# Binary cross entropy on one core: from tiles with a separate output to two fixed rings worked on in place

## The chip, the cores and the metric

The kernel runs on one core of a Trainium2 chip. Time is the device time of one execution in microseconds (us), median of ten runs; the profile is one further look at a single execution. The engines that matter are VectorE (DVE), ScalarE (ACT), GpSimd (POOL, here only the issuer of transfers), SyncE (SP, the issuer of a few) and the 16 DMA engines between HBM and SBUF.

## The reference

```python
"pred":   np.random.uniform(0.01, 0.99, (8192, 8192)).astype(np.float32)
"target": np.random.randint(0, 2, (8192, 8192)).astype(np.float32)

def reference(pred, target):
    eps = 1e-7
    pred = np.clip(pred, eps, 1 - eps)
    return -(target * np.log(pred) + (1 - target) * np.log(1 - pred))
```

Every target is 0 or 1, so only one of the two logarithms counts: that of |pred + target - 1|, which is pred where the target is 1 and 1 - pred where it is 0. Both inputs and the result are float32, 268.4 MB each.

## The kernel before

The matrix is walked in 64 blocks of 128 rows, one row to an SBUF partition, 8192 columns each: a block of pred or of the result is 4.19 MB, 32 KiB in one piece per partition. Pred comes into tiles `t_p` (float32, three buffers), target into `t_t` (bfloat16, two buffers, converted on the way by the transfer), and the result leaves from `t_o` (fp16, two buffers), converted to float32 by the transfer.

For each block, `ops` issues four instructions over the whole 8192 columns: DVE forms pred - 1 + target in place (L70); ACT squares it in place (L73) and takes the logarithm in place (L74); DVE multiplies by -0.5 into `t_o` (L75). The half undoes the square. There is no clip.

The order is that of the loop. Block `bi` first issues its pred load (L116; L114 on SP for block 0) and its target load (L117) on the GpSimd queue, then the store of block `bi - 2` (L63), then its arithmetic. GpSimd issues these transfers one after another and waits ahead of each until its buffer is free: the pred load until L75 of three blocks before has read the tile, the target load until L70 of two blocks before has read the tile, the store until L75 has written `t_o`. The last two blocks go through `ops_tail` in 4 and 8 pieces (L87, L95, L96, L97), in place in `t_p`, with stores from SP (L100).

Of the kernel before, what the change touches and what calls it, by code (L numbers as in the profile page):

```python
# [1 line left out]

# [4 lines left out]


@with_exitstack
def kernel(  # L10
    ctx: ExitStack,
    tc: tile.TileContext,
    pred: bass.AP,
    target: bass.AP,
    out: bass.AP,
):
    nc = tc.nc
    fp32 = mybir.dt.float32
    fp16 = mybir.dt.float16
    bf16 = mybir.dt.bfloat16  # L20

    P = nc.NUM_PARTITIONS

    pred_f = pred.flatten_outer_dims()
    target_f = target.flatten_outer_dims()
    out_f = out.flatten_outer_dims()

    R, C = pred_f.shape

    F = 8192 if C % 8192 == 0 else C  # L30
    n_col = C // F
    n_row = (R + P - 1) // P
    n_blk = n_row * n_col

    big = (R % P == 0) and n_blk >= 8 and F == 8192

    sub = mybir.AluOpType.subtract
    add = mybir.AluOpType.add
    mult = mybir.AluOpType.mult

    Square = mybir.ActivationFunctionType.Square
    Ln = mybir.ActivationFunctionType.Ln

    pool_p = ctx.enter_context(tc.tile_pool(name="bce_p", bufs=3 if big else 2))
    pool_t = ctx.enter_context(tc.tile_pool(name="bce_t", bufs=2))
    pool_o = ctx.enter_context(tc.tile_pool(name="bce_o", bufs=2))
    pool_w = ctx.enter_context(tc.tile_pool(name="bce_w", bufs=1))

    warm = pool_w.tile([1, 8], fp32, name="warm", tag="warm")
    nc.vector.memset(warm, 1.0)  # L50
    nc.scalar.activation(out=warm, in_=warm, func=Ln)  # L51

    lb = n_blk - 1
    slb = n_blk - 2

    pending: dict[int, list] = {}

    def emit_store(b: int, n: int | None = None):
        lst = pending[b]
        n = len(lst) if n is None else n  # L60
        for _ in range(n):
            dram, sl = lst.pop(0)
            nc.gpsimd.dma_start(out=dram, in_=sl)  # L63
        if not lst:
            del pending[b]

    def ops(bi, rows, r0, g0, t_p, t_t):
        t_o = pool_o.tile([P, F], fp16, name="t_o", tag="t_o")
        p_sl = t_p[:rows]
        nc.vector.scalar_tensor_tensor(  # L70
            out=p_sl, in0=p_sl, scalar=1.0, in1=t_t[:rows], op0=sub, op1=add
        )
        nc.scalar.activation(out=p_sl, in_=p_sl, func=Square)  # L73
        nc.scalar.activation(out=p_sl, in_=p_sl, func=Ln)  # L74
        nc.vector.tensor_scalar(  # L75
            out=t_o[:rows], in0=p_sl, scalar1=-0.5, scalar2=None, op0=mult
        )
        pending.setdefault(bi, []).append(
            (out_f[r0 : r0 + rows, g0 : g0 + F], t_o[:rows])
        )  # L80

    def ops_tail(rows, r0, g0, t_p, t_t, nchunk):
        W = F // nchunk
        for k in range(nchunk):
            c0 = k * W
            p_sl = t_p[:rows, c0 : c0 + W]
            nc.vector.scalar_tensor_tensor(  # L87
                out=p_sl,
                in0=p_sl,
                scalar=1.0,  # L90
                in1=t_t[:rows, c0 : c0 + W],
                op0=sub,
                op1=add,
            )
            nc.scalar.activation(out=p_sl, in_=p_sl, func=Square)  # L95
            nc.scalar.activation(out=p_sl, in_=p_sl, func=Ln)  # L96
            nc.vector.tensor_scalar(  # L97
                out=p_sl, in0=p_sl, scalar1=-0.5, scalar2=None, op0=mult
            )
            nc.sync.dma_start(  # L100
                out=out_f[r0 : r0 + rows, g0 + c0 : g0 + c0 + W], in_=p_sl
            )

    for bi in range(n_blk):
        i, j = divmod(bi, n_col)
        r0 = i * P
        rows = min(P, R - r0)
        g0 = j * F

        t_p = pool_p.tile([P, F], fp32, name="t_p", tag="t_p")  # L110
        t_t = pool_t.tile([P, F], bf16 if big else fp32, name="t_t", tag="t_t")

        if big and bi == 0:
            nc.sync.dma_start(out=t_p[:rows], in_=pred_f[r0 : r0 + rows, g0 : g0 + F])  # L114
        else:
            nc.gpsimd.dma_start(out=t_p[:rows], in_=pred_f[r0 : r0 + rows, g0 : g0 + F])  # L116
        nc.gpsimd.dma_start(out=t_t[:rows], in_=target_f[r0 : r0 + rows, g0 : g0 + F])  # L117

        s = bi - 2
        if s in pending:  # L120
            emit_store(s)

        if big and bi == slb:
            ops_tail(rows, r0, g0, t_p, t_t, 4)
        elif big and bi == lb:
            ops_tail(rows, r0, g0, t_p, t_t, 8)
        else:
            ops(bi, rows, r0, g0, t_p, t_t)

    for b in sorted(pending):  # L130
        emit_store(b)


# [1 line left out]
_INS = ['pred', 'target']  # L135
_OUTS = [((8192, 8192), 'float32')]


# [23 lines left out]
```

## Time and profile before

| what | value |
|---|---|
| median of 10 runs | 1867.65 us (1867.37 to 1867.91) |
| the profiled execution | 1867.91 us, of which the profile's span is 1866.2 us |
| L70, DVE, 128x8192, 62 times | 8.693 us each, 538.9 us in all |
| L73 and L74, ACT, 128x8192, 62 times each | 7.029 us each, 435.8 us in all for each line |
| L75, DVE, 128x8192, float32 to fp16, 62 times | 4.427 us each, 274.4 us in all |
| a transfer's issue on GpSimd | 0.53 to 0.54 us |
| median from issue to landing | pred load 49.3 us, target load 49.0 us, store 40.2 us |

Busy time is that of the engine; the idle time that a group shows is the time of its engine just before it, with the event that ended it. DMA has no instruction rows of its own: its busy share is in the slices of the span, the rate of a stretch in the windows, and the time from issue to landing in the list of issues.

### The profile page before, as it was taken

The page shows a single profiled execution, that of the slowest core. Times are in us where ns is not written, and L with a number is a line of the kernel's source. Part 1 is how long each engine was busy: PE and PEld are TensorE (multiplying, and loading weights), DVE is VectorE, ACT ScalarE, POOL GpSimd, SP SyncE. Part 2 cuts the span into 40 slices and gives each one's busy share as a digit, 9 for nine tenths or more (in the row PEclk, how much of TensorE's full clock was granted, in tenths as well). Part 3 has the DMA queues.
Part 4 walks back from the last instruction along what each step waited for, and adds up shares of the span by engine and source line. Part 5 has one row for each costly group of instructions (what it writes and reads, how often), then busy time and mean ns, then how long its engine had stood idle before and what let it go on. Part 6 is the DMA issues. An engine that isn't in the chain of part 4 may idle for free.

```text
span 1866.2 us, 804 instructions
## 1 busy us (share of the span) xinstructions
DVE 841.3 (45%) x149; ACT 903.3 (48%) x150; POOL 100.6 (5%) x193
## 2 busy tenths in 40 slices
DVE  2545344453443534435344353453534535345353
ACT  3653644535445354453544535446354463553654
POOL 0000000000000000000000000000000000000000
DMA  9999999999999999999999999999999999999999
GB/s 326 337 376 354 349 381 343 376 358 345 386 339 376 355 347 383 346 367 363 343 388 346 363 369 340 391 340 363 370 344 386 345 359 371 347 379 352 352 379 350
DMA packets 29094, 671.14 MB, mean 360 GB/s; under 512 B 3233, under 2 KB 3233, under 8 KB 4257
## 3 DMA queue, kind: packets, MB, share of 16 engines
q0 software_dynamic: 27216, 658.52, 99.9%
q1 hardware_dynamic: 1872, 12.58, 1.7%
q14 instruction: 6, 0.04, 0.0%
HBM read 536.87 MB, written 268.44 MB: 432 GB/s over the span
## 4 chain that ended last, share of the span: by engine, by line
DMA 81%; issue 15%; ACT 2%; DVE 1%; another core or an unknown queue 1%; POOL 0%; POOLq 0%; DVEq 0%; PEldq 0%
DMA t_t<-in_target_dram 81%; ACT t_p L96 1%; ACT t_p L95 1%; DVE t_p L70 0%; DVE t_o L75 0%; DVE t_p L87 0%; DVE t_p L97 0%; POOL t_p L116 0%; POOL t_t L117 0%; POOL out_dram L63 0%; POOLq L117 0%; POOLq L63 0%; DVEq L87 0%; DVEq L70 0%
## 5 line engine op out<-in xcount | busy, mean ns | idle before, releaser
L73 ACT ACTIVATE t_p<-t_p 128x8192 f32<-128x8192 f32 x62 | 435.8, 7029 | 924.1 <-DVE t_p L70 924.1
L75 DVE TENSOR_SCALAR t_o<-t_p 128x8192 f16<-128x8192 f32 x62 | 274.4, 4427 | 845.0 <-ACT t_p L74 845.0
L70 DVE SCALAR_TENSOR_TENSOR t_p<-t_p,t_t 128x8192 f32<-128x8192 f32 x62 | 538.9, 8693 | 145.3 <-DMA t_t<-in_target_dram 145.3
L74 ACT ACTIVATE t_p<-t_p 128x8192 f32<-128x8192 f32 x62 | 435.8, 7029 | 2.0
L63 POOL DMA_DIRECT2D out_dram<-t_o x62 | 33.3, 537 | 1122.3 <-DVE t_o L75 1101.7
L117 POOL DMA_DIRECT2D t_t<-in_target_dram x64 | 34.0, 531 | 581.8 <-DVE t_p L70 581.0
L116 POOL DMA_DIRECT2D t_p<-in_pred_dram x63 | 33.8, 536 | 0.3 <-issue 0.3
L95 ACT ACTIVATE t_p<-t_p 128x1024 f32<-128x1024 f32 (+1 forms) x12 | 15.6, 1328 | 26.5 <-DVE t_p L87 26.5
L87 DVE SCALAR_TENSOR_TENSOR t_p<-t_p,t_t 128x1024 f32<-128x1024 f32 (+1 forms) x12 | 18.4, 1575 | 17.2 <-DMA t_t<-in_target_dram 17.2
L96 ACT ACTIVATE t_p<-t_p 128x1024 f32<-128x1024 f32 (+1 forms) x12 | 15.6, 1330 | 0.1
L97 DVE TENSOR_SCALAR t_p<-t_p 128x1024 f32<-128x1024 f32 (+1 forms) x12 | 10.3, 869 | 7.9 <-ACT t_p L96 7.9
L51 ACT ACT_TABLE_LOAD x1 | 1.3, 1283 | 0.7 <-PEq L146 0.7
L50 DVE MEMSET warm<- 1x8 f32 x1 | 0.1, 65 | 0.8 <-PEq L146 0.8
L51 ACT ACTIVATE warm<-warm 1x8 f32<-1x8 f32 x1 | 0.2, 207 | 0.0
L146 POOL MEMSET const-float32-0.0<- 128x1 f32 x1 | 0.1, 100 | 0.3 <-issue 0.3
L146 POOL MEMSET const-bfloat16-1.0<- 128x1 bf16 x1 | 0.1, 102 | 0.0
L146 POOL MEMSET const-float32-1.0<- 128x1 f32 x1 | 0.1, 100 | 0.0
L146 POOL MEMSET const-uint8-127<- 128x1 uint8 x1 | 0.1, 100 | 0.0
## 6 DMA issues: line engine op xcount, KB each, us to landing
t_p<-in_pred_dram POOLq DMA_DIRECT2D x63, 4096.0 KB, 49.3
out_dram<-t_o POOLq DMA_DIRECT2D x62, 4096.0 KB, 40.2
t_t<-in_target_dram POOLq DMA_DIRECT2D x64, 2048.0 KB, 49.0
t_p<-in_pred_dram SPq DMA_DIRECT2D x1, 4096.0 KB, 19.4
out_dram<-t_p SPq DMA_DIRECT2D x4, 1024.0 KB, 27.3
out_dram<-t_p SPq DMA_DIRECT2D x8, 512.0 KB, 8.5
```

The costliest lines, as they stand in the source:

```text
L51: nc.scalar.activation(out=warm, in_=warm, func=Ln)
L63: nc.gpsimd.dma_start(out=dram, in_=sl)
L70: nc.vector.scalar_tensor_tensor(out=p_sl, in0=p_sl, scalar=1.0, in1=t_t[:rows], op0=sub, op1=add)
L73: nc.scalar.activation(out=p_sl, in_=p_sl, func=Square)
L74: nc.scalar.activation(out=p_sl, in_=p_sl, func=Ln)
L75: nc.vector.tensor_scalar(out=t_o[:rows], in0=p_sl, scalar1=-0.5, scalar2=None, op0=mult)
L87: nc.vector.scalar_tensor_tensor(out=p_sl, in0=p_sl, scalar=1.0, in1=t_t[:rows, c0 : c0 + W], op0=sub, op1=add,)
L95: nc.scalar.activation(out=p_sl, in_=p_sl, func=Square)
L96: nc.scalar.activation(out=p_sl, in_=p_sl, func=Ln)
L97: nc.vector.tensor_scalar(out=p_sl, in0=p_sl, scalar1=-0.5, scalar2=None, op0=mult)
L116: nc.gpsimd.dma_start(out=t_p[:rows], in_=pred_f[r0 : r0 + rows, g0 : g0 + F])
L117: nc.gpsimd.dma_start(out=t_t[:rows], in_=target_f[r0 : r0 + rows, g0 : g0 + F])
```

## The change

The matrix is taken as one flat run. A chunk of width w is 128 x w consecutive elements, partition p holding w of them in a row. Widths are 4096, 4096, 8192, then 30 times 16384 (64 KiB per partition in float32), then 8192, 4096, 2048, 1024, 1024; together 524288 columns.

In SBUF there are two tiles for the whole run: `ring_p`, 32768 columns of float32, and `ring_t`, 32768 columns of bfloat16. Chunk k lies at its start column modulo 32768. The result replaces pred in `ring_p` and is stored from there as float32. All transfers but the first pred load are issued on the GpSimd queue. `load_what_fits` issues the target and the pred load of each next chunk as far as the ring has room behind the last chunk whose store was issued.

The arithmetic runs in pieces of 2048 columns (1024 in the two last chunks). `front` is clip and subtraction on DVE, Abs and Ln on ACT; `back` is a multiplication by -1 on DVE. The loop issues `front` of piece i, then `back` of piece i - 2; when that was the last piece of its chunk, it issues the chunk's store and what can be loaded then. The order on each engine is that of the loop.

```diff
+RING = 32768
+SUB = 2048
+LAG = 2
+def chunk_widths(total):
+    head = [4096, 4096, 8192]
+    tail = [8192, 4096, 2048, 1024, 1024]
+    big = 16384
...
-    pool_p = ctx.enter_context(tc.tile_pool(name="bce_p", bufs=3 if big else 2))
-    pool_t = ctx.enter_context(tc.tile_pool(name="bce_t", bufs=2))
-    pool_o = ctx.enter_context(tc.tile_pool(name="bce_o", bufs=2))
+    ring_p = pool.tile([P, RING], fp32, name="ring_p", tag="ring_p")
+    ring_t = pool.tile([P, RING], bf16, name="ring_t", tag="ring_t")
...
+    def load_t(k):
+        c, w = at(k), widths[k]
+        nc.gpsimd.dma_start(out=ring_t[:, c : c + w], in_=dram(target_f, cols[k], w))
+    def load_p(k):
+        c, w = at(k), widths[k]
+        queue = nc.sync if k == 0 else nc.gpsimd
+        queue.dma_start(out=ring_p[:, c : c + w], in_=dram(pred_f, cols[k], w))
+    def store(k):
+        c, w = at(k), widths[k]
+        nc.gpsimd.dma_start(out=dram(out_f, cols[k], w), in_=ring_p[:, c : c + w])
...
-        nc.vector.scalar_tensor_tensor(
-            out=p_sl, in0=p_sl, scalar=1.0, in1=t_t[:rows], op0=sub, op1=add
-        )
-        nc.scalar.activation(out=p_sl, in_=p_sl, func=Square)
-        nc.scalar.activation(out=p_sl, in_=p_sl, func=Ln)
-        nc.vector.tensor_scalar(
-            out=t_o[:rows], in0=p_sl, scalar1=-0.5, scalar2=None, op0=mult
-        )
+    def front(c, w):
+        p, t = ring_p[:, c : c + w], ring_t[:, c : c + w]
+        nc.vector.tensor_scalar(
+            out=p, in0=p, scalar1=EPS, scalar2=1 - EPS, op0=Alu.max, op1=Alu.min
+        )
+        nc.vector.scalar_tensor_tensor(
+            out=p, in0=t, scalar=1.0, in1=p, op0=Alu.subtract, op1=Alu.add
+        )
+        nc.scalar.activation(out=p, in_=p, func=Act.Abs)
+        nc.scalar.activation(out=p, in_=p, func=Act.Ln)
+    def back(c, w):
+        p = ring_p[:, c : c + w]
+        nc.vector.tensor_scalar(
+            out=p, in0=p, scalar1=-1.0, scalar2=None, op0=Alu.mult
+        )
...
+    def load_what_fits():
+        nonlocal loaded
+        while (
+            loaded < len(widths)
+            and cols[loaded] + widths[loaded] <= (cols + [total])[stored] + RING
+        ):
+            load_t(loaded)
+            load_p(loaded)
+            loaded += 1
+    with tc.manual_schedule():
+        load_what_fits()
+        nc.vector.memset(warm, 1.0)
+        nc.scalar.activation(out=warm, in_=warm, func=Act.Ln)
+        for i in range(len(pieces) + LAG):
+            if i < len(pieces):
+                _, c, w, _ = pieces[i]
+                front(c, w)
+            if i >= LAG:
+                k, c, w, last = pieces[i - LAG]
+                back(c, w)
+                if last:
+                    store(k)
+                    stored = k + 1
+                    load_what_fits()
```

## The prediction

> **What bounds the kernel now.** I read the page first, from the totals to the engines.
>
> ```profile
> span 1866.2 us, 804 instructions
> DVE 841.3 (45%) x149; ACT 903.3 (48%) x150; POOL 100.6 (5%) x193
> DMA  9999999999999999999999999999999999999999
> q0 software_dynamic: 27216, 658.52, 99.9%
> HBM read 536.87 MB, written 268.44 MB: 432 GB/s over the span
> ```
>
> DVE and ACT are busy for less than half of the span; the 16 DMA engines are full in every slice. The reads and writes of HBM add up to 805.3 MB, and no byte of that can go: the two inputs and the result are float32 on the HBM side. So the limit is the flow of transfers, and what counts in the change is whether the flow is ever interrupted. Next, the windows of one undisturbed stretch (its length, the busy time of DVE, ACT and GpSimd, the clock, the DMA share and the rate) and the timeline of a block (start, length, engine and line, and in brackets the idle time before it with what ended that) give the rate and the rhythm:
>
> ```profile
> 1748.11:1806.12 58.01, 26.24 (x5) 28.12 (x4) 2.65 (x5) 1.00 1.02 361
> ```
> ```profile
> 758.50 0.54 POOL L63 DMA_DIRECT2D out_dram<-t_o  x1 [18.05 <-DVE t_o L75]
> 759.03 0.54 POOL L116 DMA_DIRECT2D t_p<-in_pred_dram  x1
> 759.98 8.69 DVE L70 SCALAR_TENSOR_TENSOR t_p<-t_p,t_t 128x8192 f32<-128x8192 f32 x1 [1.77 <-DMA t_t<-in_target_dram]
> 768.70 7.03 ACT L73 ACTIVATE t_p<-t_p 128x8192 f32<-128x8192 f32 x1 [14.95 <-DVE t_p L70]
> 768.96 0.53 POOL L117 DMA_DIRECT2D t_t<-in_target_dram  x1 [9.39 <-DVE t_p L70]
> ...
> 782.82 4.43 DVE L75 TENSOR_SCALAR t_o<-t_p 128x8192 f16<-128x8192 f32 x1 [14.16 <-ACT t_p L74]
> 787.54 0.54 POOL L63 DMA_DIRECT2D out_dram<-t_o  x1 [18.06 <-DVE t_o L75]
> 789.03 8.69 DVE L70 SCALAR_TENSOR_TENSOR t_p<-t_p,t_t 128x8192 f32<-128x8192 f32 x1 [1.78 <-DMA t_t<-in_target_dram]
> ```
>
> A block starts every 789.03 - 759.98 = 29.05 us; over the long stretch 29.03. It carries 3 x 4.19 MB on the HBM side, so 12.58 MB / 29.03 us = 433 GB/s (the window's 361 counts the target at its two bytes in SBUF). All 64 blocks at this pace are 64 x 29.03 = 1857.9 us of the 1866.2. The rest is the start (the window view shows the first packets at about 1.75 us), the way from the last packet to the end (the rate collapses near 1863.1, so 3.1 us), and some 3.5 us of small losses. The timeline also shows why there is no hole: the table "us to landing" puts a target load at 49.0 us from issue to landing although its share of the flow is below 10 us, so transfers stand in line well ahead of the engines. Last, the groups by shape give prices for 2048 columns:
>
> ```profile
> L87 DVE SCALAR_TENSOR_TENSOR t_p<-t_p,t_t 128x2048 f32<-128x2048 f32 x4 | 9.0, 2287 | 1.7 <-DMA t_t<-in_target_dram 1.7
> L95 ACT ACTIVATE t_p<-t_p 128x2048 f32<-128x2048 f32 x4 | 7.5, 1898 | 8.5 <-DVE t_p L87 8.5
> L97 DVE TENSOR_SCALAR t_p<-t_p 128x2048 f32<-128x2048 f32 x4 | 4.9, 1226 | 4.7 <-ACT t_p L96 4.7
> ```
>
> **What the Trainium skill says.** "DMA: Bandwidth & Descriptors", section Where 436 GB/s comes from, puts the ceiling of one core's transfers at 435.2 GB/s; the 433 here agrees, so longer runs have nothing left to win. The same page, Latency and other measured facts, warns of lost rate at row pitches of large powers of two, but its table still has full rate at 512 KiB (207 of 214 GB/s); the change goes from 32 to 64 KiB. The trace shows only 32 KiB and below. "SBUF — State Buffer", section SBUF: two separate sides, says that GpSimd can't write the descriptors of its transfers while a two-port VectorE instruction runs, and that such a transfer starts after that instruction. Before, no store is issued inside such an instruction, so this trace doesn't show it.
>
> **The change, part by part.**
>
> 1. Bytes. The store now reads float32 in SBUF in place of fp16, but wrote float32 to HBM before too. The side that limits stays 4 bytes per element: 805.3 MB as before. Change 0; by the ceiling at best 1857.9 - 805.3/0.4352 = 7.5 us could be won, and I take 0.
>
> 2. Compute. Per piece of 2048 columns DVE does clip, subtract and negate. The clip is a new form; it has one source as L97 has, so I take 1.226 us (if it ran at one element per cycle as L87 does, 2.287). Sum 1.226 + 2.287 + 1.226 = 4.74 us, for 256 pieces 1213 us. ACT: 2 x 1.90 = 3.80 us, 973 us; Abs is priced as Square. Both stay below the 58.06 us that the flow needs per 16384 columns: DVE 8 x 4.74 = 37.9, ACT 30.4. Hidden, as throughput. The activation table is still loaded once.
>
> 3. Buffers. Before, three pred tiles, two target tiles and two separate outputs let loads run on while a block is computed and stored. After, the pred ring holds 32768 columns, that is two big chunks, and the result stays in its place. Chunk k+2 can be loaded only where chunk k was, after its store. The target load of k+2 and the pred load of k+2 are issued behind store(k) on the one GpSimd queue. The pred load waits for the store to land, which costs nothing: the target load of k+2, 8.39 MB on the HBM side, takes 8.39/0.433 = 19.4 us and flows meanwhile.
>
> 4. The order on DVE, where it goes wrong. The loop issues front(i) and only then back(i-2). The last two negations of chunk k stand behind clip and subtract of pieces 0 and 1 of chunk k+1, and the first of those clips waits for the pred load of k+1. DVE runs in order. So store(k) can't be issued until load k+1 has landed, and behind store(k) stand the loads of k+2. In the moment in which load k+1 lands nothing is left in the DMA queues. The flow stops, once per chunk. Without the lag the two negations could have been done some 12 us before, since chunk k needs 37.9 us of DVE and about 8 us for its last pieces on ACT after its own load has landed, and the next three transfers take 58 us.
>
> The hole, step by step: last packet to DVE's start 1.4 us (block 0 of before: 8.39 MB for its two loads from 1.75 us take 19.35, that is to 21.1; DVE starts at 22.52). Then clip, subtract, negate, clip, subtract, negate: 2 x 4.74 = 9.5 us (hops between them are 0.02 to 0.05 in the chain of waits, and overlaps of 0.06 stand against them). DVE to GpSimd 0.3 (55.05 to 55.34). From the issue to the first packet: SP's first transfer took 1.0 us (0.75 to 1.75); the GpSimd instruction is 0.54 where SP's is 0.37, and descriptors are written by software, so 1.5, bounds 1.0 and 2.5. Then the descriptor stall: right behind the negation DVE starts the next clip, 1.226 us; bounds 0 and 2.5 (the page's stall of a short copy), taken 0.5. Sum 1.4 + 9.5 + 0.3 + 1.5 + 0.5 = 13.2 us. Bounds 12.2 (no stall, fast issue) to 16.2; with a clip at one element per cycle 2.1 more.
>
> 5. How many holes. Chunks 0 to 2 are the head (16384 columns), 3 to 32 are big, 33 to 37 are the tail. At the start chunks 0 to 3 are loaded in one go; stores 0 and 1 (4.84 us each) stand behind load 3 and cover 9.7 us of the first hole, leaving 3.5. After the loads of chunks 4 to 32 the hole is whole: 29 of them, 29 x 13.2 = 383 us. The tail has none: store(31) is followed by 38.7 us of tail loads, the first of which lands early enough for store(32), and compute of the tail (7 x 4.74 + 2 x 2.6 = 38 us) is done before its 38.7 us of stores. Short rows cost there under 1 us, as the last slices still move 414 to 426 GB/s.
>
> Sum: 1.75 + 1857.9 + 383 + 3.5 + 3.1 = 2249 us of span. The profiled execution was 1867.91 for a span of 1866.2, 1.7 more, and the median 1867.65 is within 0.3 of it. So 2251. Where before had 3.5 us of small losses, I keep none; that is inside the range.
>
> **Rivals.**
>
> A (forecast, 0.80): holes of 12 to 15 us per chunk, about 2250.
>
> B (0.10): larger holes, because the clip isn't as quick as L97 (2 x 1.06 = 2.1 us a hole) or descriptors wait longer behind DVE. For it: neither is in the trace. Against: the clip has one source and both sides in SBUF as L97. 29 x 2.1 = 61 us give 2312; with a stall of 2 us more, 2370.
>
> C (0.05): runs at 64 KiB pitch flow slower. At 5% of 1858 us, 93 more: 2344. Nothing in the trace speaks for it; the skill's table speaks against.
>
> D, the other side (0.05): the hole is covered, and the kernel is no slower. That happens if the store of chunk k reaches the queue before load k+1 has landed, so that the DMA engines always have a transfer: then 1.75 + 1857.9 + 3.1 + 1.7 = 1864 us, or to 1868 with the old losses. It decides at a place, the last negation of a chunk: 12 us earlier and the hole is gone. For it: all the work needed is ready (spare DVE time 20 us per chunk). Against: the negation stands behind a clip that waits for that load, in one in-order queue. A faster flow can't do it: the chunk would have to pass in 58.06 - 13.2 = 44.9 us, at 561 GB/s.
>
> **How the numbers follow.** The likeliest is A, 2251. The range takes its bounds, 12 us (29 x -1.2 = -35, and up to 7.5 from a flow at the ceiling) and 15.5 us (+67), so 2205 to 2320; this takes in the first half of B. What a measurement can tell from no change is about 0.2%, 4 us. D splits between faster and same: faster 0.02, same 0.03, slower 0.95.
>
> **What would show it.** In the changed profile: DMA slices of 8 and fewer tenths, mean busy share near 1860/2249 = 83%; in the timeline each big store on GpSimd about 10 us after DVE's first clip of the next chunk; a cycle of 58.1 + 13.2 = 71.3 us from store to store; the clip at 1.2 us. It is wrong if stores are issued before that clip starts, if the DMA row stays at 9 throughout (D), or if a window between holes moves less than 430 GB/s on the HBM side (C).

## The result, and the profile after

The changed kernel takes 2242.05 us (median of 8 runs, 2241.85 to 2242.2) against 1867.64 us: a ratio of 1.2005, 95% interval 1.1994 to 1.2015. The forecast was 2251, with a range from 2205 to 2320.

The page of the changed kernel, the same lines as were read of the kernel before:

```profile
span 2240.9 us, 1564 instructions
DVE 1172.4 (52%) x772; ACT 979.9 (44%) x516; POOL 96.5 (4%) x117
DMA  9977977789778887779877797777977889778989
q0 software_dynamic: 16272, 669.00, 84.3%
HBM read 536.87 MB, written 268.44 MB: 359 GB/s over the span
```

The bytes are the same. What is new is in the DMA row: 7 and 8 where every slice had 9. No engine is fuller than the DMA engines, and yet they stand idle for a sixth of the time. So the question is not what is slow but when nobody has given them work. The timeline of one change of chunks answers it (start, length, engine and line; in brackets the idle time before and what ended it; rows of ACT and later pieces left out):

```profile
1275.84 1.23 DVE L88 TENSOR_SCALAR ring_p<-ring_p 128x2048 f32<-128x2048 f32 x1 [33.86 <-DMA ring_p<-in_pred_dram]
1277.10 2.29 DVE L91 SCALAR_TENSOR_TENSOR ring_p<-ring_t,ring_p 128x2048 f32<-128x2048 bf16 x1
1279.31 1.22 DVE L99 TENSOR_SCALAR ring_p<-ring_p 128x2048 f32<-128x2048 f32 x1
...
1280.44 1.22 DVE L88 TENSOR_SCALAR ring_p<-ring_p 128x2048 f32<-128x2048 f32 x1
...
1281.70 2.29 DVE L91 SCALAR_TENSOR_TENSOR ring_p<-ring_t,ring_p 128x2048 f32<-128x2048 bf16 x1
1283.91 1.22 DVE L99 TENSOR_SCALAR ring_p<-ring_p 128x2048 f32<-128x2048 f32 x1
...
1285.42 0.96 POOL L84 DMA_DIRECT2D out_dram<-ring_p  x1 [46.79 <-DVE ring_p L99]
...
1286.37 0.55 POOL L75 DMA_DIRECT2D ring_t<-in_target_dram  x1
...
1308.18 1.20 POOL L80 DMA_DIRECT2D ring_p<-in_pred_dram  x1 [21.26 <-DMA out_dram<-ring_p]
```

DVE has been idle for 33.86 us, with the two negations of the old chunk in line, until the pred load of the next chunk lands. Then it does clip, subtract, negate twice over, and only then, 9.58 us later, is the old chunk's store issued. GpSimd had waited 46.79 us for it. Half-microsecond windows around it show the last packets of the load beginning by 1273.5 (each lasts some 2.4 us) and no traffic to speak of until the store's first packets between 1286.5 and 1287.5:

```profile
1286.50:1287.00 0.50, 0.50 (x1) 0.50 (x1) 0.42 (x1) 1.00 2.22 918
1287.00:1287.50 0.50, 0.50 (x1) 0.50 (x1) 0.00 (x0) 1.00 2.81 1180
```

The last two numbers are the DMA share and the rate. A window counts a packet where it begins, with its whole length, so the share can pass 1. Read packet by packet, the trace has the last packet of the load ending at 1275.4 and the first of the store beginning at 1286.95: a standstill of 11.5 us, and the same to 0.1 us in all 29 whole holes.

The windows show what a cycle costs (its length, busy DVE, ACT and GpSimd, the clock, the DMA share, the rate); the first is a whole cycle, the second lies between two holes:

```profile
1237.42:1308.18 70.76, 36.63 (x25) 30.59 (x17) 2.71 (x3) 1.00 0.84 296
...
1217.00:1274.00 57.00, 24.80 (x17) 23.05 (x13) 1.21 (x1) 1.00 0.99 350
```

Between the holes the engines are full; over the cycle their share is 0.84. A cycle of 70.76 us against 58.06 makes a hole of 12.7 us: the 11.5 us of standstill, and 1.2 us more that are lost while packets flow.

### The profile page after: what moved, and what is told of

Read it like the earlier page. It is cut to its first block, busy times and chain, and to the rows that moved or that the text cites. A ratio compares the mean times of both kernels' runs of the same rounds, so it can differ in the third digit from the quotient of the medians.

```text
span 2240.9 us, 1564 instructions
## 1 busy us (share of the span) xinstructions
DVE 1172.4 (52%) x772; ACT 979.9 (44%) x516; POOL 96.5 (4%) x117
## 4 chain that ended last, share of the span: by engine, by line
DMA 54%; issue 28%; DVE 14%; POOL 2%; another core or an unknown queue 1%; POOLq 0%; DVEq 0%; PEldq 0%
DMA ring_p<-in_pred_dram 52%; DVE ring_p L91 7%; DVE ring_p L88 4%; DVE ring_p L99 3%; DMA out_dram<-ring_p 2%; POOL out_dram L84 1%; POOL ring_t L75 1%; POOLq L164 0%; POOL ring_p L80 0%; POOLq L84 0%; DVEq L88 0%; PEldq L164 0%
## 5 line engine op out<-in xcount | busy, mean ns | idle before, releaser
L94 ACT ACTIVATE ring_p<-ring_p 128x2048 f32<-128x2048 f32 (+1 forms) x257 | 489.5, 1905 | 1227.3 <-DVE ring_p L91 1227.1
L88 DVE TENSOR_SCALAR ring_p<-ring_p 128x2048 f32<-128x2048 f32 (+1 forms) x257 | 313.0, 1218 | 1033.1 <-DMA ring_p<-in_pred_dram 1033.1
L91 DVE SCALAR_TENSOR_TENSOR ring_p<-ring_t,ring_p 128x2048 f32<-128x2048 bf16 (+1 forms) x257 | 587.0, 2284 | 10.0 <-DMA ring_t<-in_target_dram 1.2
L95 ACT ACTIVATE ring_p<-ring_p 128x2048 f32<-128x2048 f32 (+1 forms) x257 | 489.0, 1903 | 8.1
L99 DVE TENSOR_SCALAR ring_p<-ring_p 128x2048 f32<-128x2048 f32 (+1 forms) x257 | 312.5, 1216 | 0.5 <-ACT ring_p L95 0.5
L84 POOL DMA_DIRECT2D out_dram<-ring_p x38 | 34.8, 916 | 1477.4 <-DVE ring_p L99 1477.1
L80 POOL DMA_DIRECT2D ring_p<-in_pred_dram x37 | 40.4, 1092 | 638.1 <-DMA out_dram<-ring_p 617.0
L75 POOL DMA_DIRECT2D ring_t<-in_target_dram x38 | 21.7, 572 | 5.3 <-DMA ring_t<-in_target_dram 4.5
```

What stands on the lines that cost most here:

```text
L75: nc.gpsimd.dma_start(out=ring_t[:, c : c + w], in_=dram(target_f, cols[k], w))
L80: queue.dma_start(out=ring_p[:, c : c + w], in_=dram(pred_f, cols[k], w))
L84: nc.gpsimd.dma_start(out=dram(out_f, cols[k], w), in_=ring_p[:, c : c + w])
L88: nc.vector.tensor_scalar(out=p, in0=p, scalar1=EPS, scalar2=1 - EPS, op0=Alu.max, op1=Alu.min)
L91: nc.vector.scalar_tensor_tensor(out=p, in0=t, scalar=1.0, in1=p, op0=Alu.subtract, op1=Alu.add)
L94: nc.scalar.activation(out=p, in_=p, func=Act.Abs)
```

## The experiments

All are edits of the changed kernel. Two theories stand against each other at the start: that the hole comes from the order on DVE (the lag), or that a ring of two chunks worked on in place, or its 64 KiB runs, is slow in itself.

**The negations ahead of the next chunk's clips.** The lag stays inside a chunk; at its end the last two negations are issued at once.

```diff
-        for i in range(len(pieces) + LAG):
-            if i < len(pieces):
-                _, c, w, _ = pieces[i]
-                front(c, w)
-            if i >= LAG:
-                k, c, w, last = pieces[i - LAG]
-                back(c, w)
...
+        waiting = []
+        for piece in pieces:
+            k, c, w, last = piece
+            front(c, w)
+            waiting.append(piece)
+            while waiting and (last or len(waiting) > LAG):
+                _, cb, wb, _ = waiting.pop(0)
+                back(cb, wb)
...
```

> The lag theory: the hole of about 12 us per chunk comes only from the two negations that stand on DVE behind the first clips of the next chunk. With the negations of a chunk's last two pieces issued ahead of the next chunk's first clip, each store is issued some 10 us before the next load lands, all 29 holes go (29 x 12.7 = 368 us), the DMA row shows 9 throughout, and the time is 2242 - 368 - 4 = about 1870 us (1864 to 1876). The depth theory (two chunks in a ring filled in place are too few, whatever the order): the time stays above 2150 us. The run-length theory (64 KiB per partition flow slower): between 1900 and 2000 us with no holes.

Measured: 1873.36 us (1872.35 to 1874.13), ratio to before 1.003 (1.0019 to 1.0041). Of the 374 us lost, 369 are back. The DMA row of its page, and its timeline:

```profile
DMA  9999999999999999999999999999999999999997
```
```profile
1169.31 0.54 POOL L84 DMA_DIRECT2D out_dram<-ring_p  x1 [17.98 <-DVE ring_p L99]
...
1188.34 1.23 DVE L88 TENSOR_SCALAR ring_p<-ring_p 128x2048 f32<-128x2048 f32 x1 [19.33 <-DMA ring_p<-in_pred_dram]
...
1207.93 1.35 POOL L80 DMA_DIRECT2D ring_p<-in_pred_dram  x1 [37.55 <-DMA out_dram<-ring_p]
...
1227.27 0.54 POOL L84 DMA_DIRECT2D out_dram<-ring_p  x1 [17.99 <-DVE ring_p L99]
```

The store (1169.31) now stands 19 us ahead of the landing that DVE waits for (1188.34), where it came 9.6 us after it. DVE still waits, for 19.33 us, but nothing hangs on that. The cycle is 1227.27 - 1169.31 = 57.96 us. The same ring, the same clip and the same 64 KiB runs thus flow at full rate: the depth and run-length theories fall.

**Half the chunk, same lag.**

```diff
-    big = 16384
+    big = 8192
```

> The 62 middle chunks (60 of them new) are 8192 columns wide, so the same ring holds four; the lag of two pieces stays. The lag theory as a whole (order and depth together make the hole): while DVE waits for load k+1, loads of k+2 and k+3 are still queued for 38.7 us, so the late store leaves no hole: about 1870 us (1862 to 1880). A theory that the late negation costs its 9.2 us of DVE time per chunk wherever it stands: twice as many chunks, 1866 + 60 x 12.7 = about 2630 us.

Measured: 1877.75 us, ratio to before 1.0057 (1.0042 to 1.0072). The time is as expected, but the way to it is not. The timeline, and two lines of the list of waits (who waited for what: us in all, times, the longest):

```profile
1105.13 1.23 DVE L88 TENSOR_SCALAR ring_p<-ring_p 128x2048 f32<-128x2048 f32 x1 [10.55 <-DMA ring_p<-in_pred_dram]
1115.07 0.60 POOL L80 DMA_DIRECT2D ring_p<-in_pred_dram  x1 [27.38 <-DMA out_dram<-ring_p]
1115.66 0.54 POOL L84 DMA_DIRECT2D out_dram<-ring_p  x1
```
```profile
POOL ring_p L80 <- DMA out_dram<-ring_p: 1621.9, 59, 28.4
POOL out_dram L84 <- DVE ring_p L99: 54.7, 5, 18.8
```

The lag is still there: the last negation of the chunk ahead ends at 1114.42, behind two clips of the chunk that DVE began at 1105.13. But the store at 1115.66 is not that chunk's. Counted from the start, it belongs to the chunk before that one, whose last negation had ended at 1085.38; it stood on GpSimd behind a pred load that waited 27.38 us for an earlier store to land. Stores wait for DVE only 5 times in the whole run, where they did so 36 times, for 1477.1 us in all, in the changed kernel. And when the load lands at 1105.11, an earlier store and a target load are still under way and land at 1114.79 and 1124.41. So 19.3 us of transfers are left, not the 38.7 us of loads that were expected, and the flow goes on.

A late negation thus costs nothing where its store isn't due yet and where other transfers are still queued when the newest load lands. This run changes both at once; the run with the target load ahead of the store, further down, changes only the second. Where the 10 us against the kernel before go stays open.

**One piece of lag, and three.** `LAG = 1` and `LAG = 3` in place of 2.

> LAG is 1, so only one clip and one subtraction, and the negation of the last piece but none before it, stand ahead of the store. The lag theory: each hole loses one turn of clip, subtract and negate on DVE, 4.60 us from start to start in the trace; 29 holes and the first, partly covered one: 30 x 4.6 = 138 us less, 2104 us (2095 to 2115). A theory in which the hole is the way through the queues and not the DVE instructions: 2242 us.

> LAG is 3: one more turn of clip, subtract and negate ahead of each store, 30 x 4.6 = 138 us more than with 2, 2380 us (2368 to 2390). If the hole grew only until some other wait covers it, less than 2330 us.

Measured: 2105.98 and 2380.58 us (two executions each). From 1 to 2 to 3 the time rises by 136 and 138.5 us, 30 times 4.5 and 4.6 us. From DVE's start on the new chunk to the store's issue it takes 4.99 us with a lag of one (1132.81 to 1137.80), 9.58 with two and 14.19 with three (1203.04 to 1217.23). The hole is a straight line in the number of pieces that stand ahead of the store.

**Without the clip.** The `tensor_scalar` call that begins at L88 is left out.

> The clip is left out (the arithmetic of all other steps stays; pred lies in 0.01 to 0.99). Before each store stand two clips fewer, 2 x 1.15 us from start to start. The lag theory: 30 holes, 30 x 2.3 = 69 us less, 2173 us (2165 to 2180). If what counts were DVE's total work, 256 x 1.15 = 294 us less, 1948 us. If the hole didn't hang on DVE, 2242 us.

Measured: 2157.25 us, below the expected 2165 to 2180: 84.8 us less, where 69 were reckoned. The timeline:

```profile
1227.54 2.29 DVE L88 SCALAR_TENSOR_TENSOR ring_p<-ring_t,ring_p 128x2048 f32<-128x2048 bf16 x1 [41.12 <-DMA ring_p<-in_pred_dram]
1234.60 0.54 POOL L84 DMA_DIRECT2D out_dram<-ring_p  x1 [45.02 <-DVE ring_p L96]
...
1295.47 2.29 DVE L88 SCALAR_TENSOR_TENSOR ring_p<-ring_t,ring_p 128x2048 f32<-128x2048 bf16 x1 [41.15 <-DMA ring_p<-in_pred_dram]
```

The cycle is 67.93 us, 2.83 less, and 30 x 2.83 = 85. From DVE's start to the store's issue it is 7.06 us in place of 9.58: the two clips cost 1.26 each from start to start, because the subtraction waits for the clip's result (1275.84 to 1277.10), where 1.15 was reckoned from instructions that overlap. The other 0.3 us lie behind the issue. There the store takes 0.54 us where it took 0.96: the next DVE instruction beside it is now the subtraction and no longer the clip. DVE lost a quarter of its work, 314 us of busy time (1172.4 to 858.0), and the time only what stood ahead of the stores.

**The target load ahead of the store.**

```diff
+                    fits = (cols + [total])[k + 1] + RING
+                    while (
+                        t_loaded < len(widths)
+                        and cols[t_loaded] + widths[t_loaded] <= fits
+                    ):
+                        load_t(t_loaded)
+                        t_loaded += 1
                     store(k)
...
```

(Not shown: `load_what_fits` now skips a target load that has been issued.)

> The target load of chunk k+2 is issued ahead of store(k) in place of behind it; the lag stays. The lag theory: the target load flows for 19.4 us while DVE works through the two pieces, so the store's hole of 12.7 us is covered; but now the pred load of k+2 stands directly behind the store's landing, with nothing queued between: a new hole from the store's last packet to the pred load's first, about 0.8 (landing) + 1.4 (issue to first packet) and up to 1 more, 2.2 to 3.5 us per chunk. 1868 + 30 x 2.2 to 3.5 = 1934 to 1973 us, about 1950. A theory that any transfer queued ahead removes the whole loss: 1866 to 1872 us.

Measured: 2000.84 us, outside the expected 1934 to 1973. The timeline, and a window of one microsecond:

```profile
1140.90 1.23 DVE L88 TENSOR_SCALAR ring_p<-ring_p 128x2048 f32<-128x2048 f32 x1 [25.91 <-DMA ring_p<-in_pred_dram]
1150.48 0.96 POOL L84 DMA_DIRECT2D out_dram<-ring_p  x1 [30.61 <-DVE ring_p L99]
1181.14 0.53 POOL L80 DMA_DIRECT2D ring_p<-in_pred_dram  x1 [29.69 <-DMA out_dram<-ring_p]
```
```profile
1182.00:1183.00 1.00, 0.00 (x0) 0.00 (x0) 0.20 (x1) 1.00 3.17 1049
```

As expected, the old hole is covered, although the store still waits for the newest load (1140.90 to 1150.48), and a new hole stands elsewhere: the pred load is issued only when the store has landed, and nothing is queued between. But a cycle is 62.34 us (1118.80 to 1181.14), 4.3 over 58.06, where 2.2 to 3.5 were reckoned. The packets of the trace account for it. The store's last packets end by 1180.5 and the load's first begin at 1182.36; since the 16 engines stop and start at slightly different times, each stands idle for 2.5 us on average. The estimate had covered that much. It had left out that some packets last longer: these first packets of the load 3.2 us where 2.4 is the rule, and the last packets of the target load, begun between 1156.9 and 1157.5, 3.5 us. That is 0.8 and 1.1 us more, and the sum is the 4.3 us. The page's DMA row shows 9 in all but the last slice, since a loss of some 4 us in 62 leaves the share above 0.9; the row alone would have hidden 133 us.

**The last stores, and a version meant to beat the kernel before.** First the five tail stores go out from SP, with the early negations kept; then the negations also lag again in the tail, once all loads are issued. The edit of the stores:

```diff
-        nc.gpsimd.dma_start(out=dram(out_f, cols[k], w), in_=ring_p[:, c : c + w])
+        queue = nc.sync if k >= len(widths) - 5 else nc.gpsimd
+        queue.dma_start(out=dram(out_f, cols[k], w), in_=ring_p[:, c : c + w])
```

> As the run with the negations issued early, but the stores of the five tail chunks go out from SP. In that run the last packets ran near 1863.5 us of a span of 1872.4, 8.9 us before the end; before, with its last stores on SP, about 2 us. If stores on the GpSimd queue cost a longer end: 4 to 6 us less, about 1868 us. If the end is the same from either queue: 1873 us.

> As the run with tail stores from SP, and in the tail, once all loads are issued, the negations lag by two pieces again, so that DVE doesn't wait for ACT at the end of each small chunk. The stores there come some 10 us earlier; the flow's end is then set by the bytes alone. 1 to 3 us less than with the early negations everywhere, about 1866 us; against the kernel before, a ratio of 0.998 to 1.000.

Measured: 1869.44 us, ratio to before 1.001 (1.0003 to 1.0016), and 1868.85 us, 1.0008 (1.0002 to 1.0015). The stores from SP give 3.9 us against the first experiment. With GpSimd stores last, the flow had all but ended long before the span did, as the windows of that experiment show:

```profile
1859.00:1863.00 4.00, 0.00 (x0) 0.00 (x0) 0.53 (x1) 1.00 0.70 289
1863.00:1867.00 4.00, 0.00 (x0) 0.00 (x0) 0.00 (x0) 1.00 0.08 32
1867.00:1871.00 4.00, 0.00 (x0) 0.00 (x0) 0.00 (x0) 1.00 0.00 0
```

The last packets end at 1866.6 in that run and at 1866.9 with the tail stores from SP; the span goes on for 5.7 and for 1.2 us after them. So the gain lies behind the flow and not in it. SP's waits at the closing line are 5.2 us in the first experiment and in the changed kernel, and 0.6 us in both versions with stores from SP. The lagged tail gives 0.6 us where 1 to 3 were expected, and the intervals of the two overlap; the expected ratio of 0.998 to 1.000 was missed. No version beats the kernel before. They come within about 0.1% of it, because all flow at the same rate; over most of the run a cycle of the last one is between 57.9 and 58.9 us.

## Why the prediction was right

- **Bytes and rate (step 1)** held: 805.3 MB, and between the holes a share of 0.99. Runs of 64 KiB neither gain nor lose: 57.96 us for 16384 columns in the settled part of the first experiment, 58.06 before. This part also bears out what the Trainium skill says under "DMA: Bandwidth & Descriptors", Where 436 GB/s comes from: 25.17 MB / 57.96 us = 434 GB/s, just below its ceiling.
- **Compute hidden (step 2)** held, and the clip's price was right: 1.222 us measured, 1.226 taken from L97. DVE grew by 331 us, and the run with early negations carries that work within 0.3% of the time before.
- **Buffers (step 3)** held: the pred load of 1308.18 waits 21.26 us for the store to land, and the target load, which lands at 1327.2, flows meanwhile.
- **Order on DVE (step 4)** is the cause. The evidence is the run in which nothing but that order is changed (1873 us) and the straight line over lags 1, 2 and 3. The clip's removal shows that time follows the instructions ahead of the store and not DVE's total.
- **Size of the hole.** 13.2 us forecast, 12.7 measured, and here the sum was better than its terms. From the end of the last packet to DVE's start it is 0.4 us, where 1.4 was forecast. From there to the store's issue it is 9.58, where 9.5 + 0.3 was. From the issue to the first packet it is 1.5 with the stall in it, where 1.5 + 0.5 was. Together these make the standstill of 11.5 us, 1.7 less than the forecast. The other 1.2 us had no term: they are lost while packets flow, 0.8 of them in the last packets of each store, begun at 1304.0 to 1304.1 in the cycle shown, which last 3.2 us in place of 2.4. That two errors nearly cancel is luck. The 1.4 was not read but reckoned, from a steady rate since 1.75 us in the kernel before; in its packets the target load of block 0 ends at 22.2, which is 0.3 us before DVE starts.
- **The stall** behind a two-port instruction, of which "SBUF — State Buffer", SBUF: two separate sides, tells, was put at 0.5 us. It fits that the store's issue takes 0.96 us beside a clip and 0.54 us without, that the longer issue ends 0.1 us after that clip does (1286.38 and 1286.26), and that without the clip the first packet comes 1.1 us after the issue in place of 1.5. That the port is what it waits for was not tried apart.
- **Number of holes (step 5)** held: from store 3 at 152.76 us to store 31 at 2134.63 lie 28 cycles of 70.78 us, and a whole hole stands ahead of store 3 as well, which makes 29. Store 2, which by the prediction's terms would go out at about 90.4 us, came at 91.65.
- **What missed.** 0.5 us a hole, 14 us in all, was forecast too high. Against it the stretch from store 31 to the end was 4 us too low. Of these some 2.6 are the last step: 5.7 us from the last packet (2235.1) to the end, where 3.1 was taken from a kernel that ends with stores from SP. Another 2.2 are in the flow of the tail, 99.0 us where 96.8 were reckoned, and 0.5 go the other way.
- **Rivals.** Rival D, that the hole is covered, became true as soon as the negation moved; the place named for its decision was right. The store then went out 19 us ahead of the next landing and not 12, since DVE was done 38.6 us after its own load and the 8 us added for ACT were not needed. Rival B is refuted by the clip's 1.22 us and the stall's size. The sign named for rival C, less than 430 GB/s between holes, did come true: 25.17 MB in 70.76 - 11.5 = 59.2 us are 425 GB/s. But the rival itself is refuted, since the first experiment moves the same 64 KiB runs at 434; the loss is mostly in the one round of long packets per cycle.

## What to carry to other kernels

In a kernel bound by transfers, ask at each landing what is still in the queue; if the answer is nothing, every instruction between that landing and the next issue is paid in full, however idle its engine is on average. A software lag that delays the end of a tile behind the start of the next puts that next tile's wait ahead of the store; drain the lag at each tile's end, or see that other transfers are still queued at that landing, as smaller tiles in the same ring did here. A row of 9s in the slices can still hide small holes, so check the cycle against the bytes.

## What the runs showed of the hardware that was not expected

- With stores from GpSimd as the last transfers the end is longer: 5.7 us from the last packet to the end of the span in the first experiment, 1.2 us with the five tail stores from SP, which gave 3.9 us of time. SP's wait at the closing line fell from 5.2 to 0.6 us. What takes that time was not tried.
- Some packets of a transfer last longer than the usual 2.4 us: 3.2 us for the last 64 KiB packets of each store in the changed kernel, and in the run with the target load first 3.5 us for the last packets of the target load and 3.2 us for the first of the pred load after the standstill. A standstill alone doesn't do it: after the 11.5 us in the changed kernel the store's first packets last 2.5 us. In the first experiment's cycle from 1169.31 to 1227.27 no packet lasts longer than 2.44 us; there the 16 engines begin their packets spread over 2 us, in the other two runs within 0.1 to 1.0 us of each other. Whether that is the reason was not tried.
- An issue on GpSimd is stretched beside a clip or a negation: in the changed kernel 65 of the 67 that fall into one end 0.12 us after it and last up to 1.4 us, as the store of 1285.42 (0.96 us) and the pred load of 1308.18 (1.20 us). The issues beside the subtraction take 0.54 to 0.57 us.
- A DVE instruction that needs the result of the one ahead starts 1.26 us after it where an independent one starts 1.13 to 1.14 us after (a 1.22 us clip or negation): the wait costs the overlap too. The kind of instruction is not the reason, since without the clip the same subtraction starts 1.13 us after an independent negation (1229.75 to 1230.88).
